# Half-height products of attention scores and mLSTM states, widened to all 128 rows with zeros

## The chip, the cores and the metric

The kernel runs on one core of a Trainium2 chip. The metric is the device time of one execution in microseconds (us). Several runs are taken, and their median counts. The core has a matrix engine (TensorE, PE in the profile; its weight loads are shown apart as PEld), VectorE (DVE), ScalarE (ACT), GpSimd (POOL) and SyncE (SP), which issues the DMAs.

## The reference

Two blocks are computed one after the other, for 256 latent tokens and 256 context tokens of 1024 features. The first block has two layers, each a mixer (pooling, a gating unit and neighbourhood attention of eight heads of 64 features, gated and added) and an MLP. The second block has an mLSTM layer and a layer of sliding-window attention (16 query heads, four key heads of 64 features), each with an MLP. The parts that this change touches are the scores and the state products:

```python
# neighbourhood attention (first block), one row of queries
s_win = einsum('bhqd,biqjhd->bhqij', q_row, k_win) * scale + bias
s_ctx = einsum('bhqd,bchd->bhqc', q_row, k_ctx) * scale
p = softmax(concatenate([s_win, s_ctx], -1))
# windowed attention (second block)
s_lat = where(valid, einsum("bqhgd,bkhd->bhgqk", qb, kb) * scale, -inf)
s_ctx = einsum("bqhgd,bchd->bhgqc", qb, ck) * scale
# mLSTM, one direction, chunks of 128 tokens: c0 is the state before a chunk
wq = exp(d - m_t) * einsum("bhctd,bhcsd->bhcts", q_c, k_c)
num = einsum("bhcts,bhcse->bhcte", wq, v_c) + carry_w * einsum("bhctd,bhcde->bhcte", q_c, c0)
```

Inputs and results are 32-bit floats.

## The kernel before, in words

Everything large is a product of three matrix instructions: a number is split into a high part, rounded to the matrix engine's 32-bit form (`F32R`), and a low part, the rest; high times high, high times low and low times high are summed in PSUM. Features lie on the partitions, tokens on the columns (0 to 255 context, 256 to 511 latents). The program is laid out by a scheduler: it takes the instructions in the order written, with priorities, and gives each engine a fixed order. Tiles of a tag share a number of slots (`SLOTS`, line 89): 16 for A and for B, 4 for Y, 2 for G and E, 12 for Q, 3 for W. A tile waits until a slot of its tag is free.

The stages in order: the first layer's start, projections and attention (to about 250 us), its gates, output product and MLP (to about 850), the second layer (850 to 1325; its attention stands at 920 to 985), the mLSTM (1325 to 1600), its MLP (to about 1950), the windowed attention (to about 2115) and the last MLP. While an attention stage waits for its softmax, products of the next projection or of the gates are issued in between.

**Scores.** A head has 64 features, so two heads share the 128 partitions; `HALF` names the two halves. `put_q` (line 714) writes, for each head `hh` of a pair, the high part of q into its own half and the low part into the other half of `q[:, hh]`. `put_k` (line 707) writes the high part of k into both halves of `kh[hh]`, and the low part into the head's own half of a tile `kl` that the two heads share. `score` (line 720) then needs two instructions: one over all 128 rows (q high and q low times k high) and one, called the low product here, over the head's 64 rows (q high times k low):

```python
self.mm(S, q[:, hh, c], kh[hh][:, :n], stop=False)
self.mm(S, q[r, hh, c], kl[r, :n], start=False)
```

It is called for 128 queries at a time: in the first block for each of four head pairs and two query tiles against 512 keys, in both layers, and in the first layer for the context queries against 256 keys too; in the windowed attention for eight pairs. What follows a score tile (`attend_lat`, line 725) is a chain: the maximum and the biased scores on DVE, the exponential on ACT, the division on DVE, four transposes on PE, a copy on ACT to W, and the weighing of the values on PE (`weigh`, line 776, two heads side by side in 64 columns each).

**States.** In the mLSTM, `heads` (line 1166) goes over four heads and two directions. For each of them ACT and DVE make `qs`, the scaled queries of the head, in the head's 64 partitions of an E tile, and W, the weights within a chunk. For each chunk with a state before it (three of four) `pn` is the sum of W times the values (128 rows) and `qs` times the state `Cs` over the head's 64 rows (line 1203). Both are 32-bit products without a split; each takes two instructions on the engine. The state tile has the two heads of a pair one above the other.

POOL does part of the modulation (sums over weights' rows, line 449), parts of the norms (adds, and the power -1/2 at lines 522 and 1225) and of the rotations (line 692).

Of the kernel before, what the change touches and what calls it, by code (L numbers as in the profile page):

```python
# [12 lines left out]
F32 = mybir.dt.float32  # L13
# [17 lines left out]
# pieces of modulation work per column tile, in each layer's mixer and mlp  # L31
RATES = ((1.4, 2.0), (0.7, 0.0), (1.4, 1.8), (0.0, 0.0))
# how many row tiles each of a group's column tiles is behind the one before
SKEW = 2
# after how many row tiles the parts of other work are issued: the second half of the very first
# modulation, those of a norm among a product's first and last ones, and those of one that a
# product doesn't wait for
# [3 lines left out]
# how many instructions sooner than its place a product's result is taken up  # L41
# [3 lines left out]
class Steps:  # L45
    """Work in parts, each to be issued when a product has come so many row tiles far."""
# [16 lines left out]
class Builder:  # L63
    def __init__(self, tc, io, stack):
# [6 lines left out]
        # the engine for the low parts of weights  # L71
# [15 lines left out]
    # Tiles of a tag go round its slots in program order. A and B hold the operands of the  # L87
    # large products in turn, Q a mixer's own operands.
# [17 lines left out]
    @contextmanager  # L106
    def sooner(self, n):
        """What is issued inside goes before what was issued up to n instructions earlier,
        on an engine that could do either."""
        self.tc.cur_priority -= n  # L110
        yield
        self.tc.cur_priority += n

# [19 lines left out]
    def staged(self, ap, n, tags):  # L133
        """A weight's tile as it comes; where Y is not in use it can stage them too."""
        tag = next(tags)
        if tag == "Y":
            raw = self.t("Y", (P, n))
        else:
            raw = self.wp.tile([P, n], F32, tag=tag, bufs=self.STAGES[tag],
                               name=self.name(tag))  # L140
        self.nc.sync.dma_start(raw, ap)
        return raw
# [19 lines left out]
    def rows_of(self, pss, tiles, ks_of, xs, r0, r1, a, e, steps=None, strict=False):  # L162
        """Row tiles r0 to r1 of column tiles, each a little behind the one before; `strict`
        keeps their order and that of the parts of `steps` on the tensor engine."""
# [22 lines left out]
    def group(self, tiles, ks_of, xs, cols, evac, steps=None):  # L187
        """Column tiles side by side, row tile by row tile, one range of tokens after the
        other."""
# [6 lines left out]
    def take(self, pss, tiles, a, e, evac):  # L196
        """Has the results of a group taken up; what can wait is put off."""
# [6 lines left out]
    def gemm(self, aps, xs, c0, evac, head=0, tail=0, order=(LAT, CTX), pre=None, mid=None, flush=True):  # L204
        """Column tiles of a product. The first `head` and the last `tail` of them go stream
        by stream; the parts of `pre` are issued in the course of the first ones' first
        stream, those of `mid` in the course of the last ones' second."""
# [25 lines left out]
    def flush(self):  # L233
        """What products left to be done when the next one's matmuls are under way."""
        late, self.late = self.late, []
        for part in late:
            part()
# [9 lines left out]
    def gemm2(self, aps, xs, c0, evac, tail=0, mid=None):  # L247
        """As gemm, for four row tiles, two column tiles to an array."""
# [14 lines left out]
    def gemm_rows(self, aps, n, xs, banks, evac, between=None, c0=0):  # L263
        """A product with the tokens on the partitions: n columns for each tile of tokens, from
        weights that come by row tiles side by side; `between` is called halfway."""
# [54 lines left out]
    def start(self, ws):  # L320
        """The first layer's first norm, its modulation by halves of the features, and as far
        as they go the products of four column tiles; `ws` are these tiles' weights, for each
        half two column tiles to an array. Returns what finishes them, too."""
# [86 lines left out]
    def mod_out(self, i, cgs, f0, ps):  # L410
        """Four row tiles of mod, from sums in rows 32 g and 32 g + 1 (the two streams)."""
# [15 lines left out]
    def mod_units(self, i, groups):  # L427
        """Columns of the modulation of layer i (for both streams) from its weights' rows, in
        pieces to be mixed with other work: products and sums over row tiles on the engines
        with time to spare, the sum over the partitions on the tensor engine."""  # L430
        w, sc = self.io[f"wmod{i}"], self.silu[i // 2]

        def unit(cg, half, k):
            raw = self.staged(w[cg, k][:, half * 512:half * 512 + 512], 512, cycle(["mraw"]))
            a0, a1 = self.macc[:, 0], self.macc[:, 1]
            # each stream has its sums, or where only the latents are modulated, these have both
# [33 lines left out]
    def drip(self):  # L470
        """Some of the pending modulation work."""
# [9 lines left out]
    def need(self, i, cg):  # L481
        """Everything pending up to a column group of layer i."""
# [4 lines left out]
    def scales(self, i, which):  # L487
        """The factor norm_gain * (1 + scale) and the shift of a layer's first or second norm."""
# [13 lines left out]
    def square(self, k, c0, c1, slot=None, adder=None, **kw):  # L502
        """Adds a row tile's squares to the running sums of one stream, the last one apart."""
# [9 lines left out]
    def rstd_rows(self, s):  # L513
        """1 / rms over the features, for a stream's tokens, the same in every partition."""
# [24 lines left out]
    def norm_twice(self, xs, A, S):  # L539
        """For the latents, in parts: their norm with the gain `fin`, and its modulated norm,  # L540
        which has one more such factor 1 / rms and `fin` in A."""
# [18 lines left out]
    def plain_xs(self, A, S):  # L560
        """For a product that is to begin before a norm of the latents is known: high and low
        parts of the residual times A, and in two columns more of the shift S (as the norm's
        factor 1 / rms belongs to a token, it can come after the product); and what takes up a
        row tile of the residual."""
# [14 lines left out]
    def norm(self, xs, s, A, S, keep=None):  # L579
        """Modulated norm of a stream's residual into the high and low parts xs, in parts;  # L580
        `keep` gets the rows of 1 / rms."""
# [27 lines left out]
    def add_to_h(self, g, squares=True, gain=None, then=None):  # L609
        """`gain` asks for the squares of the latents times it too, `then` is called with each  # L610
        row tile."""
# [15 lines left out]
    def mlp(self, i, xs, c0, tag, pre=None, mid=None, before_last=None, gain=None, plain=None):  # L627
        """`plain` (see plain_xs) and the rows of 1 / rms: the first product begins with these."""
# [58 lines left out]
    def rope(self, dst, src, perm, tab):  # L687
        """Rotates the 256 latent tokens of a tile of two heads."""
# [7 lines left out]
    def to_tokens(self, src, dst, c0):  # L696
        """Feature-major [128, tokens] to token-major columns dst(tile) [128, 128]."""
# [7 lines left out]
    # For scores, q of a head: high and low parts one above the other (the high one in its own  # L705
    # half); k of a head: the high part in both halves, the low one in its own.
    def put_k(self, kh, kl, c, src):
        for hh in range(2):
# [3 lines left out]
            self.nc.vector.tensor_sub(kl[r, c], src[r], kh[hh][r, c].bitcast(F32))  # L712
# [816 lines left out]
```

## Time and profile before

| | |
|---|---|
| median of 3 runs | 2331.84 us (2328.53 to 2334.13) |
| profiled execution, first to last instruction | 2329.3 us (no other time is shown for it) |
| PE busy | 2228.5 us (96%), 13402 matrix products |
| PEld busy | 1864.1 us (80%) |
| DVE / ACT / POOL busy | 1620.0 / 1148.6 / 681.5 us |
| DMA | 336.78 MB, 145 GB/s on average |

PE's busy time counts each product from its start to its modelled end. Products overlap, so a busy PE says that something was under way, not that it ran at its best; the distance of one start to the next says what a product cost.

### The profile page before, as it was taken

To read this page: it belongs to the slowest core of one execution; us is meant where nothing else is said; L and a number is where in the kernel's file an instruction comes from. 1 tells how busy PE (TensorE), PEld (TensorE's weight loads), DVE (VectorE), ACT (ScalarE), POOL (GpSimd) and SP (SyncE) were. 2 spreads that over 40 slices of the span, in tenths; PEclk is the share of its full clock that TensorE was granted. 3 is DMA by queue.
4 is the path that set the end of the run, shared out by engine and by line. 5 is a ranking of instruction groups with operands and counts; after the bars stand their busy time and mean duration, and the time that the engine had idled before them with its cause. 6 is when DMAs were issued, how large, how long until landed. Compare 5 with 4: busy or idle time off the path is not lost.

```text
span 2329.3 us, 36255 instructions
## 1 busy us (share of the span) xinstructions
PE 2228.5 (96%) x13402; PEld 1864.1 (80%) x13402; DVE 1620.0 (70%) x2762; ACT 1148.6 (49%) x2122; POOL 681.5 (29%) x530
## 2 busy tenths in 40 slices
PE   6899999999999999999999899999999999998998
PEld 3776777787777787798899867778777778768998
DVE  4876656677666885778877755678776566687766
ACT  3455434454443455655544645555443433665453
POOL 1540434524221542045300504154432222423001
PEclk9999999999999999999999999999999999999999
DMA  7351345445655443366554313254555532214552
GB/s 271 128 156 61 124 148 167 133 136 179 193 190 167 144 151 110 113 209 209 190 185 149 114 55 104 86 165 134 157 189 182 167 119 72 82 37 136 191 184 98
DMA packets 128145, 336.78 MB, mean 145 GB/s; under 512 B 14944, under 2 KB 24160, under 8 KB 127968
## 3 DMA queue, kind: packets, MB, share of 16 engines
q1 hardware_dynamic: 127968, 334.46, 44.5%
q8 instruction: 106, 1.74, 0.3%
q14 instruction: 71, 0.58, 0.1%
HBM read 333.36 MB, written 1.05 MB: 144 GB/s over the span
## 4 chain that ended last, share of the span: by engine, by line
PE 47%; DVE 6%; issue 2%; ACT 2%; POOL 2%; DMA 1%; DVEq 0%; POOLq 0%; SPq 0%; ACTq 0%
PE mm L122 27%; PE mx L122 11%; PE S L122 3%; PE num L122 2%; PE T L122 1%; PE pv L122 1%; PE T L126 1%; DVE wlo L130 1%; DMA mraw<-wmod_in 1%; DVE T L119 1%; DVE macc L119 1%; ACT whi L116 1%; POOL macc L449 1%; DVE A L119 1%; DVE B L119 0%
## 5 line engine op out<-in xcount | busy, mean ns | idle before, releaser
L122 PE MATMUL mm<-A,whi 128*128 128x256 f32 (+1 forms) x2600 | 666.2, 344 | 17.5 <-ACT A L116 7.6
L449 POOL TENSOR_TENSOR macc<-macc,mraw 128x512 f32<-128x512 f32 x244 | 363.3, 1489 | 697.0 <-ACT mraw L116 688.6
L122 PEld LDWEIGHTS mm<-A,whi 128*128 128x128 f32 x2600 | 446.7, 191 | 88.5 <-issue 18.8
L122 PE MATMUL mm<-B,whi 128*128 128x256 f32 (+1 forms) x1884 | 456.8, 333 | 8.4 <-DVE T L659 4.2
L122 PE MATMUL mm<-A,wlo 128*128 128x256 f32 (+1 forms) x1300 | 442.0, 340 | 0.0
L130 DVE TENSOR_TENSOR wlo<-raw,whi 128x1024 fp32r<-128x1024 f32 x252 | 344.7, 1370 | 136.4 <-ACT whi L116 134.8
L116 ACT ACTIVATE whi<-raw 128x1024 fp32r<-128x1024 f32 x273 | 287.6, 1055 | 280.7 <-PE mm L122 164.7
L122 PEld LDWEIGHTS mm<-B,whi 128*128 128x128 f32 x1884 | 319.2, 190 | 49.6 <-issue 11.1
L122 PE MATMUL mx<-A,whi 128*128 128x512 f32 (+1 forms) x1256 | 321.1, 343 | 1.6 <-ACT G L116 1.0
L116 ACT ACTIVATE mraw<-mraw,silu 128x512 f32<-128x512 f32 x244 | 175.2, 722 | 290.7 <-DVE macc L119 180.4
L122 PE MATMUL mm<-B,wlo 128*128 128x256 f32 (+1 forms) x942 | 312.1, 332 | 1.6 <-DVE wlo L130 1.6
L119 DVE SCALAR_TENSOR_TENSOR macc<-mraw,silu,macc 128x512 f32<-128x512 f32 x244 | 255.2, 1046 | 58.7 <-DMA mraw<-wmod_in 56.6
L122 PEld LDWEIGHTS mm<-A,wlo 128*128 128x128 f32 x1300 | 248.3, 191 | 28.4 <-issue 2.1
L116 ACT ACTIVATE whi<-Y 128x1024 fp32r<-128x1024 f32 x152 | 160.8, 1058 | 217.5 <-PE mm L122 145.8
L130 DVE TENSOR_TENSOR wlo<-Y,whi 128x1024 fp32r<-128x1024 f32 x148 | 192.4, 1300 | 92.2 <-ACT whi L116 92.0
L122 PEld LDWEIGHTS mx<-A,whi 128*128 128x128 f32 x1256 | 216.4, 190 | 32.0 <-issue 2.5
L122 PE MATMUL mx<-A,wlo 128*128 128x512 f32 (+1 forms) x628 | 214.9, 342 | 0.3 <-DVE wlo L130 0.3
L122 PE MATMUL mx<-B,whi 128*128 128x256 f32 (+1 forms) x836 | 201.4, 329 | 6.6 <-ACT B L116 3.3
L122 PEld LDWEIGHTS mm<-B,wlo 128*128 128x128 f32 x942 | 179.2, 190 | 21.0 <-issue 2.0
L509 POOL TENSOR_TENSOR sums<-sums,T 128x256 f32<-128x256 f32 x84 | 91.3, 1097 | 301.7 <-ACT T L116 300.2
L119 DVE SCALAR_TENSOR_TENSOR h<-mm,mod,h 128x256 f32<-128x256 f32 x278 | 125.8, 478 | 71.6 <-PE mm L122 71.3
L122 PEld LDWEIGHTS mx<-B,whi 128*128 128x128 f32 x836 | 140.9, 191 | 24.3 <-ACT B L116 3.9
(302 smaller groups left out, 3076.4 us busy)
## 6 DMA issues: line engine op xcount, KB each, us to landing
mraw<-wmod_in SPq DMA_DIRECT2D x352, 256.0 KB, 2.9
Y<-ff_in SPq DMA_DIRECT2D x152, 512.0 KB, 4.0
raw<-ff_in SPq DMA_DIRECT2D x104, 512.0 KB, 3.7
raw<-win_in SPq DMA_DIRECT2D x68, 512.0 KB, 3.6
raw<-mwin_in SPq DMA_DIRECT2D x17, 512.0 KB, 3.5
raw<-wo_in SPq DMA_DIRECT2D x16, 512.0 KB, 4.2
raw<-swin_in SPq DMA_DIRECT2D x10, 512.0 KB, 3.4
B<-wfirst_in SPq DMA_DIRECT2D x16, 256.0 KB, 5.4
```

The costliest lines, as they stand in the source:

```text
L116: return self.nc.scalar.activation(out, in_, func, **kw)
L119: return self.nc.vector.scalar_tensor_tensor(out, a, scalar, b, op0, op1)
L122: return self.nc.tensor.matmul(out, lhsT=lhsT, rhs=rhs, start=start, stop=stop, **kw)
L126: return self.nc.tensor.transpose(out, in_, self.ident[:k, :k])
L130: (eng or self.nc.vector).tensor_sub(lo, src, hi.bitcast(F32))
L449: self.nc.gpsimd.tensor_add(a1, a1, raw)
L509: (adder or self.nc.gpsimd).tensor_add(sums, sums, sq)
```

## The change

The low product of a score and the state product go over all 128 rows. The rows of the other head are multiplied by zeros: each head gets a low-key tile of its own, of which the other half is filled with zero on POOL (`low_k`, new), and the other half of `qs` is filled with zero each time that it is made. The second low-key tile of a pair takes a B slot in the first block and half of a Y slot in the windowed attention. The pooled tiles move from B to G. The diff also drops comments and docstrings.

```diff
+    def low_k(self, tiles):
+        for hh, t in enumerate(tiles):
+            self.nc.gpsimd.memset(t[HALF[1 - hh]].bitcast(F32), 0.0)
+        return tiles
+
     def put_k(self, kh, kl, c, src):
...
-            self.nc.vector.tensor_sub(kl[r, c], src[r], kh[hh][r, c].bitcast(F32))
+            self.nc.vector.tensor_sub(kl[hh][r, c], src[r], kh[hh][r, c].bitcast(F32))
...
     def score(self, S, q, c, kh, kl, hh):
-        n, r = S.shape[-1], HALF[hh]
+        n = S.shape[-1]
         self.mm(S, q[:, hh, c], kh[hh][:, :n], stop=False)
-        self.mm(S, q[r, hh, c], kl[r, :n], start=False)
+        self.mm(S, q[:, hh, c], kl[hh][:, :n], start=False)
...
         kh.append([b.t("Q", dt=F32R) for _ in range(2)])
-        kl.append(b.t("Q", dt=F32R))
+        kl.append(b.low_k([b.t(tag, dt=F32R) for tag in ("Q", "B")]))
...
-        t = b.t("B", (P, 2, L))
+        t = b.t("G", (P, 2, L))
...
                 qs = b.t("E")
+                nc.gpsimd.memset(qs[HALF[1 - h4 % 2]], 0.0)
...
-                            b.mm(pn[:, cc, :], qs[r, c * P:(c + 1) * P],
-                                 Cs[step[c] - 1][r, dr, j, :], start=False, stop=True)
+                            b.mm(pn[:, cc, :], qs[:, c * P:(c + 1) * P],
+                                 Cs[step[c] - 1][:, dr, j, :], start=False, stop=True)
...
-    kl = [b.t("Q", dt=F32R) for _ in range(2)]
+    low = b.t("Y", (P, 2, T), F32R)
+    kl = [b.low_k([b.t("Q", dt=F32R), low[:, j]]) for j in range(2)]
```

## Rows read from the trace of the kernel before

**Rows 1.** The page: span, and the chain that ended last by engine.

```profile
span 2329.3 us, 36255 instructions
...
PE 47%; DVE 6%; issue 2%; ACT 2%; POOL 2%; DMA 1%; DVEq 0%; POOLq 0%; SPq 0%; ACTq 0%
```

**Rows 2.** By tile (S, num): instructions, ns minimum/median/maximum, first and last start, shapes (rows*columns).

```profile
L122 PE MATMUL S<-Q,Y x96: 278/398/505, 168.7 to 976.4; 128*128 128x512 f32 x32, 64*128 64x512 f32 x32, 128*128 128x256 f32 x16, 64*128 64x256 f32 x16
L122 PE MATMUL S<-Q,Q x96: 272/481/502, 1369.4 to 2100.3; 64*128 64x128 f32 x32, 128*128 128x512 f32 x32, 64*128 64x512 f32 x32
...
L122 PE MATMUL num<-Q,E x96: 272/323/374, 1378.5 to 1496.0; 64*128 64x129 f32 x96
```

**Rows 3.** In order of time, windowed attention: start, duration, instruction (PE, PEld).

```profile
2029.68 0.39 PE L122 MATMUL S<-Q,Q 128*128 128x512 f32 x1
...
2029.91 0.60 PE L126 MATMUL T<-ident,E 128*128 128x128 f32 x4
...
2030.44 0.49 PE L122 MATMUL S<-Q,Q 64*128 64x512 f32 x1
...
2030.86 0.38 PE L122 MATMUL mm<-B,whi 128*128 128x256 f32 x1
2030.96 0.19 PEld L122 LDWEIGHTS mm<-B,wlo 128*128 128x128 f32 x1
...
2031.08 0.28 PE L122 MATMUL mm<-B,wlo 128*128 128x256 f32 x1
...
2031.20 0.40 PE L122 MATMUL mx<-B,whi 128*128 128x256 f32 x2
```

**Rows 4.** In order of time, mLSTM, PE.

```profile
1388.17 0.49 PE L122 MATMUL num<-Q,E 64*128 64x129 f32 x2
1388.58 0.49 PE L122 MATMUL num<-Q,W 128*128 128x129 f32 x2
```

**Rows 5.** In order of time, second layer's attention, PE.

```profile
957.94 0.81 PE L122 MATMUL S<-Q,Y 128*128 128x512 f32 x2
958.68 1.09 PE L122 MATMUL pv<-W,B 128*64 128x128 f32 x14
```

**Rows 6.** Windows: length; PE, PEld, DVE, ACT, POOL busy (instructions); clock, DMA share, GB/s.

```profile
174.00:252.00 78.00, 78.00 (x478) 52.96 (x477) 49.34 (x157) 45.42 (x109) 3.50 (x3) 1.00 0.19 62
920.00:985.00 65.00, 63.31 (x461) 49.83 (x459) 46.61 (x133) 38.02 (x78) 5.61 (x6) 1.00 0.36 115
1368.00:1412.00 44.00, 44.00 (x250) 31.43 (x250) 26.53 (x103) 25.57 (x87) 0.00 (x0) 1.00 0.09 30
1995.00:2112.00 117.00, 112.58 (x793) 84.83 (x792) 85.22 (x275) 73.42 (x176) 31.91 (x19) 1.00 0.18 59
```

**Rows 7.** Chain by line in three windows: 920 to 985, 1452 to 1497, 1995 to 2112.

```profile
by line: PE mm L122 24.8%; PE pv L122 16.6%; PE S L122 15.9%; PE T L126 11.9%; PE mx L122 6.1%; issue 3.4%; PE T L122 1.7%; ACT whi L116 1.6%; ACT Y L116 1.2%; ACT E L116 1.2%; ACT W L116 0.7%; ACT T L116 0.6%; ACT G L116 0.4%
...
by line: PE num L122 41.4%; PE mm L122 23.7%; PE T L122 11.3%; PE S L122 7.2%; PE kv L122 6.5%; DVE wlo L130 2.7%; ACT W L116 2.5%; ACT E L116 2.2%; DVE B L119 1.4%; issue 0.8%; DVE sm L1206 0.4%; DVE sm L1210 0.4%; DVE sm L1208 0.4%; DVE s
...
by line: PE mm L122 21.3%; PE S L122 18.2%; PE pv L122 16.1%; PE T L126 11.8%; PE mx L122 8.1%; DVE T L694 4.6%; issue 3.1%; PE T L122 2.4%; DVE E L743 2.1%; POOL wlo L130 2.0%; DVE Q L119 1.8%; ACT E L116 1.5%; DVE S L731 1.2%; ACT Q L116 
```

**Rows 8.** Waits, 1368 to 1412: who for whom, us in total, times, longest.

```profile
ACT E L116 <- PE num L122: 8.2, 5, 2.4
```

**Rows 9.** Groups on POOL by shape: count, busy us, mean ns, idle before.

```profile
L906 POOL TENSOR_TENSOR B<-Y,icnt 64x512 f32<-64x512 f32 x2 | 2.9, 1456 | 0.1
...
L839 POOL MEMSET Y<- 128x8 f32 x6 | 0.5, 102 | 4.8 <-PE acc L122 4.8
```

**Rows 10.** In order of time, POOL, 844 to 1416; idle before in brackets.

```profile
844.88 0.88 POOL L522 TENSOR_TENSOR sm<-sm,m 128x2 f32<-128x2 f32 x1 [1.96 <-DVE sm L521]
...
1414.79 1.02 POOL L1225 TENSOR_TENSOR sm<-sm,m 128x4 f32<-128x4 f32 x1 [51.27 <-DVE sm L1224]
```

**Rows 11.** By tile (B), 96 to 140 us: ns minimum/median/maximum, first and last start.

```profile
L130 DVE TENSOR_TENSOR B<-B,B x2: 694/900/1106, 100.4 to 103.8; 128x512 fp32r<-128x512 f32 x2
...
L116 ACT ACTIVATE B<-S x2: 597/598/600, 132.9 to 133.8; 128x512 f32<-128x512 f32 x2
```

## The prediction, made before the result was known

> **What bounds the kernel now.** I read the page's chain of waits first. Matrix products set the end over most of the span, and the weight load beside them is nearly as busy [rows 1]. So a microsecond taken from TensorE (PE) counts wherever the chain runs through it, and only there. The next view was the one by tile, to find the products that the change touches: 32 and 32 score products of 64 rows by 512 columns (latent queries), 16 of 64 by 256 (context queries), and 96 state products of 64 by 129, two instructions to each product, so 48 products [rows 2]. Then came the instructions in order of time, where only the starts of PE's count, since their ends are modelled. The last views were the windows and the chain of the stages in which these products stand: the first layer's attention (174 to 252 us), the second layer's (920 to 985), the mLSTM's two halves (1368 to 1412 is the first) and the windowed attention (1995 to 2112). In all of them the clock is granted in full (its level of 2.4 GHz) and PE is busy 96% to 100% [rows 6].
>
> **What one half-height product costs.** A full-height score product of 512 columns takes 0.23 us from its start to the next one's (2029.68 to 2029.91), one of 256 columns 0.12 us (2031.08 to 2031.20) [rows 3]. In the same rows a half-height low product stands alone. The four transposes ahead of it take 0.53 us, where four next to their like take 0.44 (0.11 each): 0.09 too much. The low product takes 0.42 us instead of 0.23: 0.19 too much. The product of 256 columns behind it takes 0.22 instead of 0.12: 0.10 too much. Together that is 0.38 us for going into the half-height form and out of it again, 0.19 a crossing. In the mLSTM pairs of 129 columns alternate between the two forms, and a pair takes 0.41 us [rows 4]; at 0.11 an instruction it would be 0.22, again 0.19 for one crossing. I take 0.197, between that and the 0.2 that 0.42 a pair would give, as starts are cut to 0.01.
>
> **How many crossings go.** A low score product between full-height products has two, a state product two: 80 x 2 + 48 x 2 = 256 at most. Following PE's instructions in order of start, 18 of the 80 low products have a weighing product (128 rows by 64 columns) on one side, as in [rows 5], where the second S product is the low one. There the crossing into the 64-column form stays, and one goes instead of two. That leaves 238: 64 - 10 = 54 in the first layer's attention, 32 - 5 = 27 in the second's, 64 - 3 = 61 in the windowed attention, 96 in the mLSTM. At 0.197 us they are worth 10.6, 5.3, 12.0 and 18.9 us, 46.9 in all with the digits cut here. A widened product streams the same columns, so nothing is added for it on PE. The mLSTM's own scores (64 rows by 128 columns, line 1176) stay as they are.
>
> **What of it reaches the end.** In the first layer's attention the chain view has no piece, so I go by PE's busy time, 78.00 of 78 us [rows 6], and count all 10.6. In the others PE's share of the chain is in [rows 7]: 24.8 + 16.6 + 15.9 + 11.9 + 6.1 + 1.7 = 77% in the second layer, 41.4 + 23.7 + 11.3 + 7.2 + 6.5 = 90% in the mLSTM (its second half), 21.3 + 18.2 + 16.1 + 11.8 + 8.1 + 2.4 = 78% in the windowed attention. That gives 4.1, 17.0 and 9.4 us, with the first 41.1.
>
> When PE is quicker, the engines that feed it have less time. VectorE's (DVE's) share would rise to 49.34 / 67.4 = 73%, 46.61 / 59.7 = 78%, 26.53 / 34.5 = 77% and 85.22 / 105 = 81% in the order of the stages; ScalarE (ACT) stays below that [rows 6]. None is full, and in the mLSTM it is ACT that waits for PE's state products [rows 8]. But each head's softmax is a chain over PE, DVE and ACT, so some of the freed time will turn into short waits. Their cost lies between nothing and all that the score stages gain (10.6 + 4.1 + 9.4 = 24.1 us). I take a tenth of the sum, 4.1 us, since the wait points at PE and no engine gets beyond 81%. What is late next in these stages is a DVE or ACT step of the same softmax.
>
> **What is added.** There are 36 fills with zero on GpSimd (POOL), 64 rows by 512: eight for the keys of each of the first two attention layers, four for the windowed one, 16 for the mLSTM's scaled queries. No fill of that size is in the trace. From below, 128 x 8 took 0.10 us; from above, an operation of two inputs on 64 x 512 took 1.46 us [rows 9]. I take 0.7, as a fill reads nothing. In the mLSTM the queue that they join is empty: POOL idles 51.27 us before the norm's power at 1414.79 [rows 10], and the cover is ACT's exponentials and DVE's product on the other half of the same tile. There the price is nothing. Without that cover it would be 16 x 0.7 = 11 us, at most 16 x 1.46 = 23. The fills of the keys go into POOL's gaps ahead of each attention stage, long before the first score. Without the gaps, eight of them would stand before the power at 844.88 [rows 10] that the second layer's first norm waits for: 8 x 0.7 = 5.6 us, at most 11.7. I take nothing and keep the 11.7 for the range.
>
> The rest is moves. The second key tile of a pair lies in the B ring and holds four of its 16 slots until the scores are done, and the pooled tiles go to G for that. The values that need those slots are written from 132.9 us on (first layer), and the gating tiles that they replace are read for the last time from 103.8 us on, which leaves a cover of 28 us [rows 11]; without it, each microsecond that the values come later would be one of PE's. In the windowed layer one Y slot is taken from the start to the last score; the weights staged there are gone by then, and the next user, the residual for the MLP, comes after the scores. No DMA is added or moved, on SP's queue or another. I put these at nothing.
>
> **The sum.** 41.1 - 4.1 = 37.0 us off the span of 2329.3 gives 2292.3. The profiled execution shows no time but its span; the median of the runs is 2.5 us above that, so I add 2.5: 2295 us.
>
> **Rivals.**
> *Waits take the place.* The score stages keep their length because two score banks and the softmax chain set their pace, and only the mLSTM gains: 2329.3 - 17.0 + 2.5 = 2315. For it speak DVE's 81% in the windowed attention and that 22% of the chain there is not PE's; against it, PE's full share in the first layer.
> *The load of a widened product stays in the open.* Its full-height load would have to wait for the product ahead, about 0.10 us for each of 176 instructions (the excess of the product behind the low one in [rows 3]): 17.6 us, 15.8 after the tenth, so 2311. Against it, the weights of a product of 128 rows start to load at 2030.96 while another of 128 rows streams, 0.12 before their own product [rows 3]. The Trainium skill, TensorE: Matmul & The Clock Gate, section Part 3 (Packing small matmuls), says that a weight load overlaps a running matmul only when their row groups differ. By that rule a load over all rows would always be in the open, and this rival's time would come out; the trace does not agree, as the row at 2030.96 shows.
> *It doesn't do what it says.* The crossings are not what costs; 2332. Against it, the same price stands in two stages with different products around.
> *Slower.* In the mLSTM the fill waits in POOL's queue behind work that waits itself, and the state product waits for the fill, 16 times. It decides from (37.0 + 4.7) / 16 = 2.6 us a step that nothing hides. At 3 us: 2295 + 48 = 2343. A fill of the dearest price (1.46) alone gives 2318. Against it, POOL's 51 idle us there.
>
> **How the numbers follow.** Forecast 0.68, waits 0.19, open load 0.05, nothing 0.05, slower 0.03. The range goes from the whole 46.9 us (2285) and 2 us for a luckier order of issue, 2283, to the waits' 2315 and 1 more, 2316, which also holds the forecast with eight dear fills in the open (2307). It leaves out about 1 in 10. A difference under 0.2% (4.7 us) could not be told from none, as the three runs lie 5.6 us apart. Faster by more than that: 0.92; within: 0.05; slower: 0.03.
>
> **What would show it.** Right: the groups of 64 rows by 512, 256 and 129 are gone and appear as 128 rows; in the mLSTM a pair next to a pair takes 0.22 us; a lone low score takes 0.23 us; the stages are 68, 61, twice 36 and 107 us long, or up to a tenth of the gain longer, and the rest is as before. Waits rival: PE has new idle time before T and S with DVE or ACT named, in the windowed attention above all. Open load: 0.33 us for a widened product of 512. Slower: PE idles before the state products, released by POOL. The prediction is wrong if stages without such products change their length, for then the order of issue has changed, which can't be read from here.

## The result, and the profile after

The changed kernel takes 2289.61 us (median of four runs, 2283.43 to 2295.85), the kernel before 2330.48 in the same session. The ratio is 0.9824, with a 95% interval of 0.9803 to 0.9844: 40.9 us faster. The forecast was 2295, the range 2283 to 2316. A second measurement of the same kernel, on another occasion, gave 2293.35 against 2332.15 (0.9834, 0.9819 to 0.9849): 38.8 us. The profiled execution is 41.7 us shorter than that of before.

The page after, with the span and the chain by engine, answers to [rows 1]:

```profile
span 2287.6 us, 36316 instructions
...
PE 44%; DVE 7%; issue 3%; ACT 2%; POOL 1%; DMA 1%; DVEq 0%; POOLq 0%; ACTq 0%; SPq 0%
```

The products by tile, as in [rows 2]:

```profile
L122 PE MATMUL S<-Q,Y x72: 275/393/502, 164.3 to 960.8; 128*128 128x512 f32 x48, 128*128 128x256 f32 x24
L122 PE MATMUL S<-Q,Q x80: 272/393/710, 1353.9 to 2061.0; 128*128 128x512 f32 x48, 64*128 64x128 f32 x32
...
L122 PE MATMUL num<-Q,E x96: 273/275/275, 1362.8 to 1464.1; 128*128 128x129 f32 x96
```

The 64-row forms of 512, 256 and 129 columns are gone (24 low products stand under S<-B,Y and 16 under S<-Y,Q now, after the tile that holds their keys). The median duration of a state product's instruction fell from 323 to 275 ns.

In order of time, a low product between transposes and a product of 256 columns in the windowed attention, as in [rows 3], and state products in the mLSTM, as in [rows 4]:

```profile
2004.97 0.60 PE L126 MATMUL T<-ident,E 128*128 128x128 f32 x4
2005.32 0.48 PE L122 MATMUL S<-Y,Q 128*128 128x512 f32 x1
2005.64 0.28 PE L122 MATMUL mx<-B,wlo 128*128 128x256 f32 x1
2005.76 0.40 PE L122 MATMUL mx<-B,whi 128*128 128x256 f32 x2
...
1373.64 0.39 PE L122 MATMUL num<-Q,E 128*128 128x129 f32 x2
1373.86 0.61 PE L122 MATMUL num<-Q,W 128*128 128x129 f32 x4
```

Four transposes, the low product and the next one take 2005.76 - 2004.97 = 0.79 us; in [rows 3] the same sequence takes 2031.08 - 2029.91 = 1.17. The two instructions of a state product take 0.22 us (1373.64 to 1373.86) instead of 0.41.

The stages in the window view, cut at the same products that stand at the ends of the forecast's stages (of the 13402 products on PE only 22 changed places, all in one stretch at 1958 to 1961 us, ahead of the windowed attention), as in [rows 6]. The last row is the middle of the windowed attention alone:

```profile
169.10:238.30 69.20, 68.97 (x478) 51.79 (x478) 50.38 (x159) 45.73 (x111) 3.64 (x3) 1.00 0.24 76
908.50:969.60 61.10, 58.99 (x460) 49.68 (x460) 46.45 (x133) 37.85 (x79) 5.62 (x6) 1.00 0.38 122
1352.50:1388.80 36.30, 36.08 (x250) 27.89 (x249) 25.80 (x102) 25.09 (x86) 3.63 (x7) 1.00 0.11 36
1962.50:2072.80 110.30, 103.09 (x793) 86.12 (x792) 85.75 (x276) 73.72 (x177) 32.06 (x19) 0.98 0.21 68
1990.00:2040.00 50.00, 48.01 (x371) 38.44 (x369) 45.56 (x150) 38.72 (x97) 15.66 (x10) 1.00 0.16 53
```

| stage | before | forecast | after | measured again |
|---|---|---|---|---|
| first layer's attention | 78.0 | 68 | 69.1 | 69.1 |
| second layer's attention | 65.1 | 61 | 61.1 | 61.1 |
| mLSTM, first half | 44.0 | 36 | 36.3 | 36.3 |
| mLSTM, second half | 45.2 | 36 | 36.7 | 36.7 |
| windowed attention | 117.1 | 107 | 110.3 | 109.3 |

The stages gave 8.9 + 4.0 + 7.7 + 8.5 + 6.8 = 35.9 us (36.9 the second time). The other 5.8 us of the profiled execution's 41.7 came from elsewhere: 4.9 of them lie ahead of the first stage, which begins at 169.1 us instead of 174.1. The chain by line shows what the windowed attention lost; the row answers to the third of [rows 7]:

```profile
by line: PE mm L122 16.3%; PE pv L122 13.9%; PE S L122 11.1%; PE T L126 10.6%; PE mx L122 7.0%; DVE E L750 5.0%; DVE T L694 4.6%; DVE Q L119 4.2%; issue 4.2%; DVE S L738 2.9%; DVE T L693 2.3%; PE T L122 2.2%; POOL wlo L130 2.2%; DVE sm L737
```

PE's share of that chain fell from 78% to 61%. The division of the softmax (line 750, 743 before) went from 2.1% to 5.0%, its biased maximum (line 738, 731 before) from 1.2% to 2.9%. PE's waits in this stage, after and (second fence) before:

```profile
PE S L122 <- ACT E L116: 2.6, 3, 2.2
PE T L126 <- DVE E L750: 1.8, 3, 0.9
PE S L122 <- DVE Q L119: 1.7, 1, 1.7
```

```profile
PE S L122 <- ACT E L116: 1.9, 3, 1.4
PE S L122 <- DVE Q L119: 1.6, 1, 1.6
PE T L126 <- DVE E L743: 0.6, 1, 0.6
```

4.1 us of waits became 6.1 (6.7 with two small ones). The fills on POOL, by shape, for which [rows 9] had only bounds:

```profile
L1191 POOL MEMSET E<- 64x512 f32 x16 | 8.3, 521 | 90.1 <-PE num L122 56.0 <-PE T L126 21.3 <-issue 6.6
L711 POOL MEMSET Q<- 64x512 f32 x10 | 4.9, 521 | 0.3
L711 POOL MEMSET B<- 64x512 f32 x8 | 3.9, 518 | 0.0
```

A fill takes 0.52 us, and POOL stands idle before the mLSTM's, most of the time until a state product gives the E slot back.

### The profile page after: what moved, and what is told of

Read it like the earlier page. It is cut to its first block, busy times and chain, and to the rows that moved or that the text cites. A ratio compares the mean times of both kernels' runs of the same rounds, so it can differ in the third digit from the quotient of the medians.

```text
span 2287.6 us, 36316 instructions
## 1 busy us (share of the span) xinstructions
PE 2184.0 (95%) x13402; PEld 1851.8 (81%) x13402; DVE 1623.2 (71%) x2762; ACT 1147.6 (50%) x2122; POOL 703.2 (31%) x566
## 4 chain that ended last, share of the span: by engine, by line
PE 44%; DVE 7%; issue 3%; ACT 2%; POOL 1%; DMA 1%; DVEq 0%; POOLq 0%; ACTq 0%; SPq 0%
PE mm L122 27%; PE mx L122 11%; PE S L122 2%; DVE wlo L130 1%; PE pv L122 1%; PE T L122 1%; PE T L126 1%; PE num L122 1%; DVE macc L119 1%; ACT whi L116 1%; DMA mraw<-wmod_in 1%; DVE A L119 1%; POOL macc L449 1%; DVE T L119 0%; POOL sums L509 0%
```

## The experiments

**The scores alone.** The mLSTM's state product as before:

```diff
-                nc.gpsimd.memset(qs[HALF[1 - h4 % 2]], 0.0)
...
-                            b.mm(pn[:, cc, :], qs[:, c * P:(c + 1) * P],
-                                 Cs[step[c] - 1][:, dr, j, :], start=False, stop=True)
+                            b.mm(pn[:, cc, :], qs[r, c * P:(c + 1) * P],
+                                 Cs[step[c] - 1][r, dr, j, :], start=False, stop=True)
```

> The change in the attention stages alone; the mLSTM's state products stay at 64 rows. Theory (each crossing between the forms costs 0.197 us, most of it on PE's path): the mLSTM part keeps the length that it has before, the three attention stages get shorter by the 8.9, 4 and 6.6 us that the changed kernel shows there, and the rest follows it too, so the time is that of the kernel before less 20 to 25 us. By the terms of the sum as predicted it would be 10.6 + 4.1 + 9.4 less a tenth: 21.7 us less. Rival (the score stages are paced by waits): under 8 us less.

Measured: 2307.59 against 2329.53, ratio 0.9909 (0.9895 to 0.9922), 21.9 us less. The mLSTM's halves keep 44.0 and 45.5 us; the attention stages take 69.2, 61.1 and 109.3. The terms of the forecast gave 21.7.

**The mLSTM alone.** The converse, on the kernel before:

```diff
                 qs = b.t("E")
+                nc.gpsimd.memset(qs[HALF[1 - h4 % 2]], 0.0)
...
-                            b.mm(pn[:, cc, :], qs[r, c * P:(c + 1) * P],
-                                 Cs[step[c] - 1][r, dr, j, :], start=False, stop=True)
+                            b.mm(pn[:, cc, :], qs[:, c * P:(c + 1) * P],
+                                 Cs[step[c] - 1][:, dr, j, :], start=False, stop=True)
```

> The change in the mLSTM alone; the attention stages and their slots are as before, so all that stands ahead of 1340 us has the order of the kernel before. Theory: 16 to 17 us less, 8 in each half of the mLSTM, and no shift of the other stages. The second use of this run: if the 5 us that the changed kernel gained ahead of 170 us come from its slots and fills, this kernel does not have them (its curve of starts against the kernel before is flat up to 1340 us, within 1 us); if they are a difference between two executions, the curve wanders here by as much, some 3 to 6 us.

Measured: 2314.03 against 2329.53, ratio 0.9937 (0.9921 to 0.9954), 15.5 us less; the halves take 36.3 and 36.7 us, as in the changed kernel. Up to the first state product the curve of starts stays within 0.5 us of the kernel before. By the expectation's own test that speaks for the slots and fills as the source of the 5 us ahead of 170 us; the next run and the last section speak against it. The two parts give 21.9 + 15.5 = 37.4 us, the sum of the forecast 37.0.

**Fills and moves without the widening.** The changed kernel, with its order on every engine, and the old rows in the two products:

```diff
-        self.mm(S, q[:, hh, c], kl[hh][:, :n], start=False)
+        self.mm(S, q[r, hh, c], kl[hh][r, :n], start=False)
...
-                            b.mm(pn[:, cc, :], qs[:, c * P:(c + 1) * P],
-                                 Cs[step[c] - 1][:, dr, j, :], start=False, stop=True)
+                            b.mm(pn[:, cc, :], qs[r, c * P:(c + 1) * P],
+                                 Cs[step[c] - 1][r, dr, j, :], start=False, stop=True)
```

> All 36 fills and all moves to other slots, and every engine's order as in the changed kernel, but the low products and the state products read 64 rows as before. Theory (the gain is that of the crossings, fills and moves cost nothing): the time of the kernel before, within 4 us, and the half-height prices are all back (a mLSTM pair at 0.41 us). Rival (fills and moves shift the start and the second layer's head): about 3 us less than before with 5 less ahead of 170 us and 3 more at 820 to 895 us. Rival (fills wait in POOL's queue and delay products): 6 to 40 us more than before, with PE idle behind POOL.

Measured: 2329.93 against 2329.53, ratio 1.0001 (0.9993 to 1.0010). Fills and moves cost nothing and bring nothing. Stretches shift against each other, though: the products near 90 us come 5 us later and those near 110 us are back at 2; the second layer's head (840 to 905 us) loses 2.4, and a part of it returns by 1300 us. That is one half of what the first rival said. The other half fails: at 170 us this run is 1.7 us late and not 5 early.

This run has the same order as the changed kernel measured again, product for product, so the two can be subtracted. The distance of each start to the next, summed over each widened product, the one before it and the one behind it, and over all others of the stage (here a stage reaches from one norm to the next and holds more than the attention windows above):

| stage | crossings removed | widened and neighbours | per crossing | the others |
|---|---|---|---|---|
| first layer | 54 | -10.1 us | 0.187 | -2.3 us, all of it ahead of 60 us |
| second layer | 27 | -5.6 us | 0.206 | +2.2 us (1.6 at one rotation at 889 us) |
| mLSTM | 96 | -18.2 us | 0.190 | +2.2 us |
| windowed | 61 | -11.9 us | 0.196 | +4.2 us |

Against the kernel before, the changed kernel's own profile gives 10.0, 5.0, 18.2 and 11.5 us, 44.7 in all or 0.188 a crossing. The table's 0.206 is not the form's: from 940 to 960 us the run with the fills alone ran at a granted clock of 0.91, and its second-layer attention takes 66.7 us where the same order in the kernel before takes 65.1 at 1.00. The crossings counted in order of start fell from 552 to 314, by the 238 of the forecast. In the last three stages the others take back 8.6 us; in the windowed one 1.9 of the 4.2 stand before transposes, 1.4 before the weighing products and 0.7 before scores.

**Half height kept, the low products put side by side.** On the kernel before; nothing is widened:

```diff
+    def scores(self, Ss, q, c, kh, kl):
+        n = Ss[0].shape[-1]
+        ins = self.mm(Ss[0], q[:, 0, c], kh[0][:, :n], stop=False)
+        with self.tc.issue_after(ins.ins):
+            ins = self.mm(Ss[1], q[:, 1, c], kh[1][:, :n], stop=False)
+        for hh in range(2):
+            r = HALF[hh]
+            with self.tc.issue_after(ins.ins), self.sooner(200 * hh):
+                ins = self.mm(Ss[hh], q[r, hh, c], kl[r, :n], start=False)
```

> No product is widened and nothing is filled; in the three attention stages the high products of a pair of heads are issued first and the two half-height low products, which lie in different rows, right behind each other. Only the order on PE differs from the kernel before. Theory (the crossing costs, not the half height): of the 142 crossings that the change removes in the scores about 70 go, 14 us on PE and, as the two halves' products start together (as the mLSTM's own scores do, 7 ns apart, in the trace), 32 x 0.23 + 8 x 0.12 = 8 us more; at 80% that is 17 us less than before. Without the starting together: 11 us less. Rival (a half-height product itself is slow, 0.38 us each): the time of the kernel before, within 4 us, and a low product in the middle of such a pair takes as long as a lone one.

Measured: 2333.77 against 2329.53, ratio 1.0022 (1.0012 to 1.0033); its profiled execution spans 2327.1. What was expected of the time fails, for a reason that the expectation had left out. The pairs do what was said. In order of time, high product, two low ones, then transposes:

```profile
177.24 0.82 PE L122 MATMUL S<-Q,Y 128*128 128x512 f32 x3
178.00 0.66 PE L126 MATMUL T<-ident,E 128*128 128x128 f32 x4
```

In the single starts the second low product follows the first by 3 to 4 ns in all 40 pairs, and here the pair takes 0.42 us to the transposes (0.43 in most pairs of 512 columns), as one alone does in [rows 3]. The Trainium skill, TensorE: Matmul & The Clock Gate, section Part 3 (Packing small matmuls), gives about 4 ns between the starts of products in different row groups; this trace agrees. So a half-height product is not slow by itself, and 76 crossings went. The mLSTM's own scores, which nothing changes, show the same without any new order. In the kernel before, eight of them stand one behind the other between full-height products:

```profile
1380.98 1.16 PE L122 MATMUL S<-Q,Q 64*128 64x128 f32 x8
1382.07 0.50 PE L122 MATMUL mm<-A,whi 128*128 128x512 f32 x1
```

The second starts 0.21 us after the first and the next one 0.20 after the last, but from the second on they follow each other at 0.11 us, as full-height products of 128 columns do. Only the ends of the row, where the form changes, are dear.

The expectation's error is in what reaches the end. The score products of the three attention stages take 14.0 us less from start to start (6.3, 4.3 and 3.4). But the first head's softmax begins later and both heads' begin together. PE's waits from 1986 to 2107 us of this run:

```profile
PE T L126 <- DVE E L753: 4.1, 6, 1.1
PE pv L122 <- ACT W L116: 3.8, 6, 0.7
```

The order on PE differs at 1226 places, so lengths compare only between places where both runs have done the same products: from the first score to the next norm 282.8 us instead of 283.8, over the second layer 253.0 instead of 255.1, over the windowed layer 158.1 instead of 155.1, and behind it 198.3 instead of 195.1. In the last two this execution also had the lower granted clock (0.97 and 0.96 against 0.99 and 0.97), and the profiled execution is the fastest of the eleven. So it is shown that 14 us on PE did not reach the end, and that PE waits for the softmax in the windowed layer; how much of the loss is these waits and how much the clock is not shown.

**The changed kernel once more** (no edit).

> The changed kernel once more, beside the kernel before on one chip, as the two parts alone gave 21.9 and 15.5 us, 37.4 together, and the whole 40.9. If the parts add up and the first measurement lay low: 36 to 38 us less than before, and the profile without the 4 us that it was early at 155 us against the run with the fills alone, whose order is the same. If the parts help each other: 41 us again, with those 4 us in the profile.

Measured: 2293.35 against 2332.15, ratio 0.9834 (0.9819 to 0.9849), 38.8 us less, between the two cases. The parts add up within the intervals. The profile is 2.7 us early at 155 us instead of 4.4: they have neither vanished nor come back whole (more in the last section).

**The mLSTM's fills sixfold.**

```diff
-                nc.gpsimd.memset(qs[HALF[1 - h4 % 2]], 0.0)
+                for _ in range(6):
+                    nc.gpsimd.memset(qs[HALF[1 - h4 % 2]], 0.0)
```

> The changed kernel, but each of the mLSTM's 16 fills is issued six times in a row on POOL, 6 x 0.52 = 3.1 us a step, more than the 2.6 us a step from which the slower rival decides if nothing hides it. Theory (POOL is idle there and the fills run ahead of their products): the time of the changed kernel, within 4 us. Rival (the state product waits for the fill): 16 x 2.6 = 42 us more than the changed kernel, about the time of the kernel before, with PE idle before the state products and POOL named.

Measured: ratio 0.9854 (0.9834 to 0.9873) against 0.9834 without the repeats; three times lie between 2295.69 and 2307.79; a fourth, 6511, is left out of the ratio, and its cause is not known. The median of the three is 6 us more than the changed kernel's, outside the 4 us of the theory. From the first state product's start to the last one's it takes 104.5 us instead of 101.2. So 80 fills more, 41.6 us on POOL, cost some 3 us there, not 42. No wait of PE in the mLSTM names POOL; one on a copy of ACT grew from 0.8 to 2.4 us. The slower rival is wrong, and one fill per step stays far from its point. The span of the profiled execution (2306.0) is longer by more than these 3 us; the last section shows where.

**The keys' products widened too.** In the mLSTM's `states` the products of keys and values write 64 rows each, two heads side by side. Here each is given zeros beside its 64 columns of keys, and the two add up:

```diff
-                kw = b.T1((P, 4, 64))
+                kw = b.t("G", (P, 8, 64))
+                nc.gpsimd.memset(kw.rearrange("p (a b) d -> p a b d", a=2)[:, :, 1:3, :], 0.0)
...
-                        b.mm(pc[64 * hh:64 * hh + 64, :], kw[:, 2 * p + hh, :],
-                             v1[c][:, 2 * p + hh, :])
+                        k0 = 4 * p + 2 * hh
+                        b.mm(pc, kw[:, k0:k0 + 2, :].rearrange("p a d -> p (a d)"),
+                             v1[c][:, 2 * p + hh, :], start=(hh == 0), stop=(hh == 1))
```

> The changed kernel, and the mLSTM's products of keys and values (96 instructions of 64 columns of output rows, two heads side by side in the two halves) get the full width too: zeros stand beside each head's 64 keys, and the two heads add up in one output. 12 more fills (128 x 256) on POOL. Theory (any crossing between forms costs 0.197 us): some 30 of the 52 crossings left there go, 5.9 us, but the two heads' products no longer run side by side, 24 x 0.11 = 2.6 us more: 3 us less than the changed kernel. Rival (only the half-height form is dear, half width is not): 2 to 3 us more than the changed kernel.

Measured: 2302.42 against 2332.15, ratio 0.9876 (0.9862 to 0.9891), 9 us more than the changed kernel. Neither theory's number holds, and the expectation had two errors. The crossings fell by 8 only, since the mLSTM's own half-height scores stand between these products. And 96 instructions are 48 pairs, so 48 x 0.11 = 5.3 us are lost, not 2.6. In order of time, in this run and (second fence) in the changed kernel:

```profile
1356.19 1.16 PE L122 MATMUL kv<-Q,G 128*128 128x129 f32 x8
1357.28 0.49 PE L122 MATMUL S<-Q,Q 64*128 64x128 f32 x4
```

```profile
1354.49 0.66 PE L122 MATMUL kv<-Q,T 128*64 128x129 f32 x8
1355.08 0.49 PE L122 MATMUL S<-Q,Q 64*128 64x128 f32 x4
```

Eight of them take 1.09 us wide and 0.59 at half width with the crossing in it. The new tiles add a wait: POOL stands idle for 26.4 us until such a product gives one of the two G slots back. Crossings and pairs alone would come to 5.3 - 8 x 0.19 = 3.8 us; the mLSTM's two halves are 5.1 longer (38.7 and 39.4 us). Where the rest of the 9 us comes from, and whether POOL's wait has a part in it, is not shown: PE's waits there name POOL for 0.5 us, as without the change.

**A shorter softmax.** The windowed attention leaves out its division by the sum (so its probabilities are not divided), in the kernel before and in the changed one:

```diff
-        nc.vector.reciprocal(den[:, 2:3], den[:, 0:1])
-        nc.vector.tensor_scalar_mul(e, e, den[:, 2:3])
+        if sink is None:
+            nc.vector.reciprocal(den[:, 2:3], den[:, 0:1])
+            nc.vector.tensor_scalar_mul(e, e, den[:, 2:3])
```

> The kernel before, with the windowed attention's division of the probabilities by their sum left out (32 reciprocals and 32 multiplications of 128 x 512 on DVE), so that DVE has less to do between a score and its transposes. It stands for comparison with the next run: the windowed stage (155 us from its norm's last sum to the next norm's) is to get shorter by under 6 us, as PE has the crossings to do anyway.

> The changed kernel with the same division left out. Theory (in the windowed stage a part of the 12.0 us of crossings was lost to waits for DVE and ACT, and only 6.4 came through): with a shorter softmax chain the stage is 9 to 12 us shorter than in the run with half-height products and no division. Rival (the shortfall is not in the waits, for example a crossing is cheaper there): again 6 to 7 us.

Measured, one execution each: 2330.82 and 2293.23 us (2325.29 for one of the kernel before). The stage between the two norms' last sums takes 156.0 us, not less than the 155.1 with the division, so the first expectation missed; wide it takes 148.7, 7.3 less than half height, near the rival's 6 to 7. But the widened products and their neighbours again gave 12.0 us there (0.191 a crossing), and the others took 4.7 back. So the crossing is not cheaper there, as the rival had it: the saving is lost between the other products, and less work on DVE doesn't end that. PE's waits in the stage without the division, half height and (second fence) wide:

```profile
PE T L126 <- ACT E L116: 4.6, 5, 1.4
```

```profile
PE T L126 <- ACT E L116: 8.1, 8, 2.2
```

The order was laid out anew with the shorter softmax, and the transposes moved up to the exponential. This pair therefore can't tell how much DVE's time alone is worth.

**Transposes ranked later.** The changed kernel, with 30 and with 80:

```diff
-        for b in range(4):
-            self.tr(pt[:, b, :], e[:, b * P:(b + 1) * P])
+        with self.sooner(0 if sink is None else -30):
+            for b in range(4):
+                self.tr(pt[:, b, :], e[:, b * P:(b + 1) * P])
```

> The changed kernel, with the windowed attention's transposes of the probabilities ranked 30 instructions later in PE's order (the order is written when the program is built; 13 places of the windowed stage change on PE). Theory (4 us of the windowed stage's 12 went into waits for the softmax at such transposes): 1 to 3 us of them come back, the stage between the two norms' last sums goes from 148 us to 145 to 147. Rival (the waits move on to the next thing in the order): 148 us or more.

> The same with 80 instructions instead of 30, so that more other products stand between a score and its transposes. Theory: up to 4 us come back, the stage is 144 to 147 us, and the time 2 to 4 us less than the changed kernel's. Rival: the weighing products and the next tile's scores, which stand behind the transposes, come late in turn; 148 us or more, and the time of the changed kernel or longer.

Measured: 2290.99 (0.9826, 0.9813 to 0.9840) and 2290.71 (0.9827, 0.9813 to 0.9841); the norm-to-norm stage takes 148.5 and 147.0 us, against 148.5 and 147.8 in two executions of the changed kernel. With 30 nothing comes back. With 80 it may be 1 us, and the stage cut as in the table above takes 108.0 us against 109.3 to 110.3 (its last product is not the same one there); as a time it can't be told from the changed kernel. No run is surely better than that one.

## Why the prediction was right, step by step

**The price of a crossing** was right: 0.188 us against 0.197, over 238 crossings 44.7 against 46.9. The runs with only the rows changed show that it is the form: fills and moves without it gave nothing, the same order with it the whole gain. The Trainium skill, TensorEngine Tiling (Array Packing), section Key Properties, says that changing the tiling mode drains TensorE; the cost at every change of form agrees with that. The page adds that a change of the tile alone is not meant; the half-height pair, whose second product starts 3 to 4 ns behind the first, agrees with it. That a drain is where the 0.19 us goes is not shown: weight loads that can't start early at a change of form would give the same starts.

**The count** was right to the crossing.

**PE's share and the tenth** were right as a sum: the stages gave 35.9 and 36.9 us where the forecast had 37.0. That the two lie so close owes something to luck: the price was 2 us too high in all, and more of it came through than forecast (80 to 83% instead of 79%). One by one, after the tenth, they were 9.5, 3.7, 15.3 and 8.5; measured were 8.9, 4.0, 16.2 and 6.8 to 7.8. In the first layer 0.7 us of the crossings' price lie ahead of 174 us, outside the window for which the forecast counted them. The step that was mis-sized is the allowance for waits in the windowed attention. There I read DVE's 81% as room, an average over the stage. In its middle, between nearly the same products, DVE was busy 82% before (45.30 of 55.2 us) and 91% after (45.56 of 50, in the windows after). Longer distances to the transposes, weighing products and scores took 4.2 of 11.9 us there, 35% instead of the forecast's 29% (share and tenth together, 3.5 of 12.0); in the first execution 10 us at a granted clock of 0.83 (1980 to 1990) added up to 1.7. The waits view names 2.7 of the 4.2 (6.9 us in the changed kernel measured again, 4.2 with the fills alone). The waits rival holds for this third and not for the stages as a whole. That DVE's load makes these waits is argued and not shown: without the division DVE was busy 73% there (36.36 of 50 us), and the waits stood at the exponential.

In the mLSTM 2.2 of 18.2 us went, norm to norm. Of the chain of its second half ACT's copies and exponentials of W and E have 10.0% now (6.3 and 3.7) and had 4.7% [rows 7].

**Fills and moves at nothing**: right, 0.4 us by the medians (interval -1.6 to +2.3). The price taken for a fill, 0.7 us, was 0.52, and even six a step stay almost covered.

**Open load**: wrong, as the median distance from a widened score of 512 columns to the next product is 0.24 us (64 of them), where it would have been 0.33. **Nothing** and **slower**: wrong, by the result and the sixfold fills.

**The last sign** was wrong: it said that the prediction is wrong if stages without such products change their length, for then the order of issue has changed. They did change, by up to 5 us, and the order on PE was the same there. The sum of 37.0 holds for the stages alone; the 2 to 5 us more that the medians show are not explained by it. The last section says how far this goes.

## What to carry to other kernels

Where small products of another height stand among full ones, count the crossings in the order in which the engine runs them and price one from a lone product and its neighbours: here 0.19 us, more than the product of 129 columns itself (0.11). Zeros that make the form uniform paid here, where the engine with the fills was idle and the narrow products did not run side by side. With the keys they did, only 8 crossings went, and widening lost more than it saved. And a saving on the matrix engine can end in waits for the softmax behind it: look at the busiest part of a stage, not only its average, before counting it in full.

## What had not been expected of the hardware

The same order of products doesn't run at the same clock each time, and that moves stretches by microseconds. The changed kernel, its repeat, the scores alone and five later variants have the same first 7741 products on PE; from the first norm's last sum to the next norm's they take 418.1 to 424.1 us. An example from 50 to 60 us, the changed kernel and (second fence) the scores alone:

```profile
50.00:60.00 10.00, 7.29 (x30) 5.17 (x29) 9.44 (x20) 4.36 (x10) 1.75 (x1) 1.00 0.01 2
```

```profile
50.00:60.00 10.00, 7.39 (x25) 5.51 (x26) 9.11 (x20) 4.39 (x10) 2.37 (x1) 0.83 0.01 2
```

PE is busy 7.3 and 7.4 us of the 10, and the granted clock is full in one and 0.83 in the other: for a third of the stretch at the lower of its two levels, 1.2 GHz. The run with sixfold fills shows it larger. PE is busy 4.41 of 8 us, while it waits for a norm, and then the clock stays at 1.2 GHz for 12 us, before its first repeated fill (1350.5 us):

```profile
1284.00:1292.00 8.00, 4.41 (x31) 3.91 (x31) 7.96 (x9) 5.24 (x10) 8.00 (x8) 0.91 0.60 199
1292.00:1304.00 12.00, 12.00 (x57) 12.00 (x58) 2.35 (x5) 0.86 (x2) 5.35 (x4) 0.50 0.34 106
```

Twelve us at half the clock are up to 6 us lost, ahead of any repeated fill; the changed kernel measured again lost up to 1.7 at this norm (a granted 0.83 from 1278 to 1288 us).

This also answers for the 4.9 us that the changed kernel gained ahead of 174 us. The clock of the first 165 us, before and (second fence) after:

```profile
0.00:165.00 165.00, 135.62 (x708) 98.95 (x709) 110.29 (x175) 75.42 (x145) 62.32 (x57) 0.94 0.56 187
```

```profile
0.00:165.00 165.00, 137.73 (x723) 100.07 (x724) 112.84 (x178) 77.45 (x149) 71.94 (x66) 0.96 0.57 190
```

The first score product, ahead of which nothing is widened, starts at 168.7 us before and at 164.3 after. But it starts at 165.6 to 168.9 us in the four profiles with the old key tiles and at 164.3 to 170.4 in the nine with the new ones, and the earliest of each group are those with the highest granted clock (0.95 and 0.96). So this part of the gain belongs to the execution, and no profile shows it to be the change's. The 2.5 us that the second layer's head loses (830 to 905 us) appear with the fills and moves alone too (2.4). That leaves the stages' 36 to 37 us as what the change is shown to give; the 2 to 5 us more in the medians stay open.
